# Layer norm by VectorE statistics, gated-attention scores two levels to a PSUM bank, and operand addresses uniform modulo 256

## The chip, the cores and the metric

The kernel runs on one core of a Trainium2 chip. The metric is the time of one execution on the device, in microseconds; runs are compared by their median. TensorE (PE in the profile) has two clock levels, 1.2 and 2.4 GHz; the profile gives the granted clock as a share of the higher one.

## What is computed

Two transformer blocks on 256 tokens of width 1024, in float32. The first block has three small attentions whose outputs are gated and merged, and a convolutional feed-forward network. The second has a gated linear attention (GLA), a layer norm, a dilated sliding-window attention and a second layer norm. The two parts that the change rewrites are these:

```python
def layer_norm(x, g, b):
    mu = jnp.mean(x32, axis=-1, keepdims=True)
    xc = x32 - mu
    var = jnp.mean(xc * xc, axis=-1, keepdims=True)
    return xc * lax.rsqrt(var + LN_EPS) * g + b

def gla_chunked(q, k, v, log_a):
    ...
        diff = bc[:, :, :, None, :] - bc[:, :, None, :, :]
        decay = jnp.where(causal, jnp.exp(jnp.where(causal, diff, 0.0)), 0.0)
        att = jnp.einsum('bhid,bhjd,bhijd->bhij', qc, kc, decay)
    ...

def second_block(x, ...):
    ...
        x = layer_norm(DEEPNORM_ALPHA * x + y, ln_g[layer], ln_b[layer])
```

## The kernel before

**Products.** Every large product is made of three float32r matmuls (`mm3`, L271): each operand is split into a high and a low part, and the three are high times low, low times high and high times high. Weights come from memory through one stream (`Stream`, L103): SP loads 1 MB into `raw`, ACT rounds 1024 columns into `whi` (L158) and VectorE (DVE) subtracts to get `wlo` (L159). Both have six buffers. Where a weight is the stationary operand (keys in `STILL`, L36) `wlo` begins 64 bytes into its buffer, otherwise at its start. In those stages 256 columns of activations move (`wstat`, L517, and `wpair`, L522); in `tokmm` (L798) the activation is stationary and 512 columns of weights move.

**Where operands lie.** A `whi` buffer has 4096 bytes per partition, a `wlo` buffer 4224, which is 16.5 times 256, so that successive `wlo` buffers begin at 0 and 128 modulo 256. The split activations of a stage take two buffers from `big8` (L397) of 8320 bytes, 32.5 times 256: one begins at 0 and the other at 128. With the offsets in the code the high and low parts lie, modulo 256 and counted from `whi`, at 0 and 128 for `hhi` and `hlo` (gate projections), at 128 and 0 for `mhi`/`mlo` and `x2hi`/`x2lo`, at 0 and 192 for `h2hi`/`h2lo` (feed-forward up projection), and at 32 and 224 for `x3hi`/`x3lo` (dilated attention). The feed-forward's own `fhi`/`flo` lie at 0 and 0.

**PSUM.** There are eight banks: four of tag `acc` (`acc_t`), two of tag `mm` (`mm_t`) and two of tag `at` (`at_t`). A tile of a tag waits until the tile that last had its bank has been read.

**GLA scores.** `gla_x` (L1012) makes, for a block b and a half u of the eight levels, one PSUM tile per head, which ACT turns into `E` by an exponential (L1024) and DVE multiplies with keys and queries into `Xk` and `Xq`. `gla_p` (L1034) then makes one PSUM tile for each level, and DVE copies it under a mask into `attT` (L1044, L1050). All these tiles have tag `at`. The two generators are advanced between the groups of value and gate projections (L1087 to L1104), which use `acc`. `gla_out(0)` (L1069) takes two `mm` banks.

**Layer norm.** `layer_norm` (L1157) runs over two row blocks b and two halves h of 512 columns. Its order is written out by hand in `ORD3` and `ORD4`, a letter for each step; a `Queue` issues each step of an engine behind the one before it, at high priority, so DVE works the list in order. `u` makes alpha x + y from PSUM with a row sum, `c` the mean (two small operations) and, on ACT, the sum of squares over 1024 columns, `r` adds epsilon on DVE and takes the power on GpSimd (POOL), `w` subtracts the mean and multiplies with g, `n`, `N` and `o` scale (on ACT, on DVE, and on DVE with the bias). The second norm ends the kernel: `o` is followed by the output's DMA for that half.

Of the kernel before, what the change touches and what calls it, by code (L numbers as in the profile page):

```python
# [30 lines left out]
ORD3 = "u00 u01 c0 w00 w01 r0 n00 n01 u10 u11 c1 w10 w11 r1 N10 N11"  # L31
ORD4 = "u00 u01 c0 w00 w01 r0 u10 o00 u11 c1 o01 w10 r1 w11 o10 o11"
SC_SWA = float(128.0 ** -0.5)


STILL = ("in1", "inc", "zg", "br", "up", "gla", "gk", "kvk", "sq")  # L36

# [65 lines left out]
class Stream:  # L103
# [31 lines left out]
    def _chunk(self, i):  # L135
# [13 lines left out]
        for o in range(0, n, part) if part > 0 else range(0, -part, 1024):  # L149
            m = min(part, n - o) if part > 0 else min(1024, -part - o)  # L150
            hi = self.pool.tile([128, 1024], F32R, tag="whi", name="whi", bufs=self.hlbufs)
            lo = self.pool.tile([128, 1056], F32R, tag="wlo", name="wlo", bufs=self.hlbufs)
# [78 lines left out]
def hybrid_blocks(ctx, tc, A, out, dbg=None):  # L231
# [124 lines left out]
    def junk():  # L356
        return cn.tile([128, D], BF, name="junk", tag="junk")
# [39 lines left out]
    def big8(dt, name, past=0):  # L397
        t = cn.tile([128, KK * S + 32], dt, name=name, tag="big8r", bufs=2)
        return t[:, past:past + KK * S].rearrange("p (k s) -> p k s", k=KK)

    hT = (big8(F32R, "hhi"), big8(F32R, "hlo"))
# [224 lines left out]
    yT = (p1.tile([128, 6, S], F32R, name="yhi", tag="yhi"), p1.tile([128, 6, S], F32R, name="ylo", tag="ylo"))  # L626
# [278 lines left out]
    res, _ = open_pool("res")  # L905
    ctx.callback(_)
# [9 lines left out]
    h2 = (big8(F32R, "h2hi"), big8(F32R, "h2lo", 16))  # L916
# [95 lines left out]
    def gla_x(b, u):  # L1012
# [5 lines left out]
        for h in range(4):  # L1018
            pm = at_t()
# [14 lines left out]
    def gla_p(b, u):  # L1034

        Xk, Xq = XK[b, u]
        for l in range(4):
            pp = at_t()
            if 4 * u + l < 7:
                n = 64 >> (4 * u + l)  # L1040
                late = lambda x: x.rearrange("p (g t s) -> p g t s", t=2, s=n)[:, :, 1, :]
                for h in range(4):
                    mm(pp[:, h * 64:(h + 1) * 64].rearrange("p (g s) -> p g s", s=n), Xk[:, h, l, :], late(Xq[:, h, l, :]), True, True)
                dve.copy_predicated(attT[:, 2 * b].rearrange("p h (g t s) -> p h g t s", t=2, s=n)[:, :, :, 1, :],  # L1044
                                    late(glamask[:, 4 * u + l, :])[:, None].to_broadcast([128, 4, 64 // n, n]),
                                    pp[:, 0:256].rearrange("p (h g s) -> p h g s", h=4, s=n))
                continue
            for h in range(4):
                mm(pp[:, h * 128:(h + 1) * 128], kT[:, h, b * 128:(b + 1) * 128], qT[:, h, b * 128:(b + 1) * 128], True, True)
            dve.copy_predicated(attT[:, 2 * b], glamask[:, 4 * u + l, :][:, None, :].to_broadcast([128, 4, 128]),  # L1050
                                pp.rearrange("p (h q) -> p h q", h=4))
# [105 lines left out]
    def layer_norm(x, y, grow, brow, dst, utile, order, after=None):  # L1157
# [3 lines left out]
        su, r, u, w = {}, {}, {}, {}  # L1161
        with tc.high_priority(BOOST):
            for step in order.split():
                op, b, h = step[0], int(step[1]), int(step[2:] or 0)
                c = half(h)
                if op == "u":
                    if not h:
                        su[b] = cn.tile([128, 6], F32, name="su", tag="su", bufs=2)
                        u[b], w[b] = utile(b), utile(b + 2)
                    qd.scalar_tensor_tensor(u[b][:, c], x[:, b, c], ALPHA, y[b][h], op0=OP.mult, op1=OP.add, accum_out=su[b][:, h:h + 1])  # L1170
                elif op == "c":
                    qd.tensor_scalar(su[b][:, 2:3], su[b][:, 0:1], su[b][:, 1:2], -1.0 / (32.0 * D), op0=OP.add, op1=OP.mult)
                    qd.tensor_scalar(su[b][:, 3:4], su[b][:, 2:3], -32.0, None, op0=OP.mult)
                    qa.activation(junk(), u[b], AF.Square, bias=su[b][:, 2:3], scale=1.0 / 32.0, accum_out=su[b][:, 4:5])
                elif op == "w":
                    qd.scalar_tensor_tensor(w[b][:, c], u[b][:, c], su[b][:, 3:4], grow[:, c], op0=OP.subtract, op1=OP.mult)
                elif op == "r":
                    r[b] = rstd(su[b][:, 4:5], 1, 1e-5, qd)
# [265 lines left out]
```

## Time and profile before

| what | value |
|---|---|
| median of 3 runs | 736.43 us (734.82 to 740.46) |
| the profiled execution | 733.62 us, of which its span 731.6 us |
| PE, DVE, ACT, POOL busy | 96%, 75%, 56%, 3% of the span |
| granted clock, mean | 0.986 |

The span runs from the first to the last instruction. PE's busy time counts overlapping matmuls once; their ends are modelled, so that the pace of matmuls is read from the distance of their starts.

### The profile page before, as it was taken

The page shows a single profiled execution, that of the slowest core. Times are in us where ns is not written, and L with a number is a line of the kernel's source. Part 1 is how long each engine was busy: PE and PEld are TensorE (multiplying, and loading weights), DVE is VectorE, ACT ScalarE, POOL GpSimd, SP SyncE. Part 2 cuts the span into 40 slices and gives each one's busy share as a digit, 9 for nine tenths or more (in the row PEclk, how much of TensorE's full clock was granted, in tenths as well). Part 3 has the DMA queues.
Part 4 walks back from the last instruction along what each step waited for, and adds up shares of the span by engine and source line. Part 5 has one row for each costly group of instructions (what it writes and reads, how often), then busy time and mean ns, then how long its engine had stood idle before and what let it go on. Part 6 is the DMA issues. An engine that isn't in the chain of part 4 may idle for free. (4 is left out here: it accounts for less than half of the span.)

```text
span 731.6 us, 12192 instructions
## 1 busy us (share of the span) xinstructions
PE 700.6 (96%) x4878; PEld 636.4 (87%) x4878; DVE 547.1 (75%) x933; ACT 407.1 (56%) x675; POOL 20.2 (3%) x34
## 2 busy tenths in 40 slices
PE   4999999999979999999999899999989999999995
PEld 4888888998859999998999797888879999999984
DVE  5877969898868776768566756675777689777866
ACT  3447788546548555554545774543555556555542
POOL 0001000000010000000000200001010000000000
PEclk8999999999999999999999999999999999999999
DMA  8996768677734765758554464231437755433201
GB/s 321 418 345 237 275 257 301 229 250 255 256 136 174 276 243 178 262 207 310 201 195 174 181 224 141 109 116 58 189 142 276 261 194 168 168 125 135 89 1 57
DMA packets 24600, 148.74 MB, mean 203 GB/s; under 512 B 2992, under 2 KB 3248, under 8 KB 9568
## 3 DMA queue, kind: packets, MB, share of 16 engines
q1 hardware_dynamic: 21888, 139.05, 52.1%
q0 software_dynamic: 1280, 5.18, 2.1%
q10 hardware_dynamic: 1376, 3.74, 1.5%
q8 instruction: 38, 0.62, 0.3%
q14 instruction: 18, 0.15, 0.1%
HBM read 145.86 MB, written 2.10 MB: 202 GB/s over the span
## 5 line engine op out<-in xcount | busy, mean ns | idle before, releaser
L159 DVE TENSOR_TENSOR wlo<-raw,whi 128x1024 fp32r<-128x1024 f32 (+1 forms) x193 | 231.3, 1210 | 63.1 <-ACT whi L158 63.1
L158 ACT ACTIVATE whi<-raw 128x1024 fp32r<-128x1024 f32 (+1 forms) x193 | 199.4, 1050 | 94.1 <-PE acc L262 42.5
L262 PE MATMUL mm<-h2hi,wlo 128*128 128x256 f32 x352 | 98.3, 280 | 0.0
L262 PE MATMUL mm<-h2hi,whi 128*128 128x256 f32 x352 | 98.1, 280 | 0.0
L262 PE MATMUL mm<-h2lo,whi 128*128 128x256 f32 x352 | 97.0, 282 | 0.0
L262 PE MATMUL mm<-x3hi,wlo 128*128 128x256 f32 x304 | 86.2, 285 | 0.0
L262 PE MATMUL mm<-x3hi,whi 128*128 128x256 f32 x304 | 85.1, 281 | 0.0
L262 PE MATMUL mm<-x3lo,whi 128*128 128x256 f32 x304 | 82.9, 280 | 0.0
L262 PEld LDWEIGHTS mm<-h2hi,wlo 128*128 128x128 f32 x352 | 67.0, 190 | 0.4
L262 PEld LDWEIGHTS mm<-h2hi,whi 128*128 128x128 f32 x352 | 66.9, 190 | 0.0
L262 PEld LDWEIGHTS mm<-h2lo,whi 128*128 128x128 f32 x352 | 65.1, 188 | 0.3
L262 PE MATMUL mm<-hhi,wlo 128*128 128x256 f32 x208 | 59.5, 286 | 0.5 <-DVE wlo L159 0.3
L262 PE MATMUL mm<-hlo,whi 128*128 128x256 f32 x208 | 59.2, 285 | 0.0
L262 PE MATMUL mm<-hhi,whi 128*128 128x256 f32 x208 | 58.7, 282 | 0.0
L262 PEld LDWEIGHTS mm<-x3hi,wlo 128*128 128x128 f32 x304 | 57.7, 190 | 0.0
L262 PEld LDWEIGHTS mm<-x3hi,whi 128*128 128x128 f32 x304 | 57.5, 189 | 0.0
L262 PEld LDWEIGHTS mm<-x3lo,whi 128*128 128x128 f32 x304 | 56.2, 188 | 0.0
L262 PEld LDWEIGHTS mm<-hhi,wlo 128*128 128x128 f32 x208 | 39.0, 188 | 2.5 <-PE mm L262 0.8
L262 PEld LDWEIGHTS mm<-hlo,whi 128*128 128x128 f32 x208 | 39.1, 188 | 0.8 <-issue 0.8
L262 PEld LDWEIGHTS mm<-hhi,whi 128*128 128x128 f32 x208 | 39.1, 188 | 0.6 <-issue 0.5
L445 DVE SCALAR_TENSOR_TENSOR adacc<-raw,cact,adacc 128x1024 f32<-128x1024 f32 x28 | 35.7, 1276 | 0.2
L262 PE MATMUL acc<-whi,flo 128*128 128x512 f32 x88 | 34.8, 395 | 0.0
(355 smaller groups left out, 1604.0 us busy)
## 6 DMA issues: line engine op xcount, KB each, us to landing
raw<-in_w_up_dram SPq DMA_DIRECT2D x22, 1024.0 KB, 4.9
raw<-in_w_ada_dram SPq DMA_DIRECT2D x16, 1024.0 KB, 4.9
raw<-in_swa_q_dram SPq DMA_DIRECT2D x16, 1024.0 KB, 4.9
raw<-in_w_zg_dram SPq DMA_DIRECT2D x12, 1024.0 KB, 4.9
raw<-in_w_dn_dram SPq DMA_DIRECT2D x11, 1024.0 KB, 4.7
raw<-in_w_ada_dram SPq DMA_DIRECT2D x16, 512.0 KB, 9.0
early<-in_w_in_dram SPq DMA_DIRECT2D x8, 1024.0 KB, 7.3
raw<-in_gla_vg_dram SPq DMA_DIRECT2D x8, 1024.0 KB, 5.1
```

Of the source, the lines that this page charges most:

```text
L158: i0 = nc.scalar.activation(hi[:, :m], raw[:, o:o + m], AF.Copy)
L159: i1 = nc.vector.tensor_sub(lo[:, :m], raw[:, o:o + m], hi[:, :m].bitcast(F32))
L262: return pe.matmul(o, l, r, start=start, stop=stop, skip_group_check=share)
L445: dve.scalar_tensor_tensor(a, w, c, a, op0=OP.mult, op1=OP.add)
```

## The change

1. `layer_norm` drops the row sums, the small mean operations and ACT's squares. A new step `v` runs `bn_stats` on DVE over each half of u, and `c` becomes one `bn_aggr` over the two, whose mean and variance `w` and `r` read. `ORD3` and `ORD4` are rewritten: each `u` is followed by its `v`, `r` comes ahead of the `w` steps, one N of the first norm's second block moves to ACT, and in `ORD4` both `o` of the first block come ahead of the second block's `u11`.
2. `gla_x` puts every second head's tile into an `mm` bank. `gla_p` puts two levels into one bank, the first two levels into an `at` and the others into an `mm` bank, issues all matmuls first and the masked copies after.
3. Buffer sizes become multiples of 256 bytes: `wlo` 4352, `big8` 8448, `yhi`/`ylo` 6400. High parts begin at their buffer's start, low parts of `h`, `y`, `h2` and `x3` 192 bytes (`PAST` = 48 elements) into theirs.
4. The pool `res`, which holds `x2`, is closed ahead of `p4`, so that the last stage's tiles lie lower.

```diff
-ORD3 = "u00 u01 c0 w00 w01 r0 n00 n01 u10 u11 c1 w10 w11 r1 N10 N11"
-ORD4 = "u00 u01 c0 w00 w01 r0 u10 o00 u11 c1 o01 w10 r1 w11 o10 o11"
+ORD3 = "u00 v00 u01 v01 c0 r0 w00 w01 n00 n01 u10 v10 u11 v11 c1 r1 w10 n10 w11 N11"
+ORD4 = "u00 v00 u01 v01 c0 r0 w00 w01 u10 v10 o00 o01 u11 v11 c1 r1 w10 w11 o10 o11"
+PAST = 48
-            lo = self.pool.tile([128, 1056], F32R, tag="wlo", name="wlo", bufs=self.hlbufs)
+            lo = self.pool.tile([128, 1088], F32R, tag="wlo", name="wlo", bufs=self.hlbufs)
-        t = cn.tile([128, KK * S + 32], dt, name=name, tag="big8r", bufs=2)
+        t = cn.tile([128, KK * S + 64], dt, name=name, tag="big8r", bufs=2)
-    hT = (big8(F32R, "hhi"), big8(F32R, "hlo"))
+    hT = (big8(F32R, "hhi"), big8(F32R, "hlo", PAST))
-    yT = (p1.tile([128, 6, S], F32R, name="yhi", tag="yhi"), p1.tile([128, 6, S], F32R, name="ylo", tag="ylo"))
+    yT = tuple(p1.tile([128, 6 * S + 64], F32R, name=n, tag=n)[:, q:q + 6 * S].rearrange("p (k s) -> p k s", k=6)
+               for n, q in (("yhi", 0), ("ylo", PAST)))
-    h2 = (big8(F32R, "h2hi"), big8(F32R, "h2lo", 16))
+    h2 = (big8(F32R, "h2hi"), big8(F32R, "h2lo", PAST))
...
-            pm = at_t()
+            pm = mm_t() if h % 2 else at_t()
...
+        levels = [l for l in range(4) if 4 * u + l < 7]
+        banks = [mm_t() if i else at_t() for i in range(2)]
+        for l in levels:
+            n = 64 >> (4 * u + l)
             for h in range(4):
+                o = banks[l // 2][:, l % 2 * 256 + h * 64:l % 2 * 256 + (h + 1) * 64]
+                mm(o.rearrange("p (g s) -> p g s", s=n), Xk[:, h, l, :], late(Xq[:, h, l, :], n), True, True)
...
                 if op == "u":
-                        su[b] = cn.tile([128, 6], F32, name="su", tag="su", bufs=2)
+                        st[b] = cn.tile([128, 16], F32, name="lns", tag="lns", bufs=2)
-                    qd.scalar_tensor_tensor(u[b][:, c], x[:, b, c], ALPHA, y[b][h], op0=OP.mult, op1=OP.add, accum_out=su[b][:, h:h + 1])
+                    qd.scalar_tensor_tensor(u[b][:, c], x[:, b, c], ALPHA, y[b][h], op0=OP.mult, op1=OP.add)
+                elif op == "v":
+                    qd.bn_stats(st[b][:, 6 * h:6 * h + 6], u[b][:, c])
                 elif op == "c":
-                    qd.tensor_scalar(su[b][:, 2:3], su[b][:, 0:1], su[b][:, 1:2], -1.0 / (32.0 * D), op0=OP.add, op1=OP.mult)
-                    qd.tensor_scalar(su[b][:, 3:4], su[b][:, 2:3], -32.0, None, op0=OP.mult)
-                    qa.activation(junk(), u[b], AF.Square, bias=su[b][:, 2:3], scale=1.0 / 32.0, accum_out=su[b][:, 4:5])
+                    qd.bn_aggr(st[b][:, 12:14], st[b][:, 0:12])
                 elif op == "w":
-                    qd.scalar_tensor_tensor(w[b][:, c], u[b][:, c], su[b][:, 3:4], grow[:, c], op0=OP.subtract, op1=OP.mult)
+                    qd.scalar_tensor_tensor(w[b][:, c], u[b][:, c], st[b][:, 12:13], grow[:, c], op0=OP.subtract, op1=OP.mult)
                 elif op == "r":
-                    r[b] = rstd(su[b][:, 4:5], 1, 1e-5, qd)
+                    r[b] = rstd(st[b][:, 13:14], 1, 1e-5, qd)
...
-    x3T = (big8(F32R, "x3hi", 8), big8(F32R, "x3lo", 24))
+    x3T = (big8(F32R, "x3hi"), big8(F32R, "x3lo", PAST))
...
     close_p3()
+    close_res()
     p4, close_p4 = open_pool("p4")
```

## Rows read from the trace of the kernel before

**Rows 1.** The page's head and its part 1: busy time of each engine.

```profile
span 731.6 us, 12192 instructions
PE 700.6 (96%) x4878; PEld 636.4 (87%) x4878; DVE 547.1 (75%) x933; ACT 407.1 (56%) x675; POOL 20.2 (3%) x34
```

**Rows 2.** Stretches: us, busy (x) of PE, PEld, DVE, ACT, POOL; PEclk, DMA.

```profile
224.00:404.00 180.00, 180.00 (x1299) 168.78 (x1298) 127.12 (x170) 96.33 (x137) 1.66 (x3) 1.00 0.62 225
541.00:543.00 2.00, 1.87 (x9) 1.87 (x10) 0.74 (x3) 1.14 (x4) 0.00 (x0) 0.50 0.78 244
```

**Rows 3.** Timeline of PE, up and down projections: start, duration, line, operation.

```profile
282.74 0.28 PE L262 MATMUL mm<-h2lo,whi 128*128 128x256 f32 x1
...
288.17 0.40 PE L262 MATMUL acc<-whi,flo 128*128 128x512 f32 x1
...
292.95 0.39 PE L262 MATMUL acc<-whi,flo 128*128 128x512 f32 x1
```

**Rows 4.** Chain that ended last: start, us, what (dilated attention, value projection, transposes).

```profile
438.49 5.57 PE acc L262 x24
...
601.73 0.87 PE at L1282 x8
602.61 5.67 PE mm L262 x48
```

**Rows 5.** Timeline of PE, the first block's output projection.

```profile
206.53 0.40 PE L262 MATMUL acc<-wlo,mhi 128*128 128x512 f32 x1
...
213.01 0.39 PE L262 MATMUL acc<-whi,mhi 128*128 128x512 f32 x1
```

**Rows 6.** Timeline of PE in the GLA stage; in brackets idle time before, and releaser.

```profile
447.11 0.50 PE L262 MATMUL at<-glamr,Ll 128*128 128x512 f32 x1 [1.22 <-ACT E L1024]
...
497.90 1.11 PE L262 MATMUL at<-Xq,Xk 128*128 128x64 f32 x8 [0.33 <-DVE attT L1044]
...
507.62 1.04 PE L193 MATMUL mm<-ident,sg 128*128 128x128 f32 x8
```

**Rows 7.** Chain that ended last, in the same stage.

```profile
445.16 1.28 ACT L1024
...
495.95 1.05 POOL rs L364
```

**Rows 8.** Timeline of all engines around the first layer norm's second block.

```profile
537.27 0.69 DVE L193 SCALAR_TENSOR_TENSOR lnu<-x,acc 128x512 f32<-128x512 f32 x1 [2.04 <-PE acc L262]
...
538.31 1.15 ACT L193 ACTIVATE junk<-lnu,su 128x1024 bf16<-128x1024 f32 x1 [1.86 <-DVE su L193]
...
540.00 0.55 POOL L364 TENSOR_TENSOR rs<-ms,mhalf 128x1 f32<-128x1 f32 x1 [4.92 <-DVE ms L193]
540.59 0.88 DVE L193 TENSOR_SCALAR x<-lnw,rs 128x512 f32<-128x512 f32 x2 [0.67 <-POOL rs L364]
...
541.13 1.97 PE L890 MATMUL acc<-ident,x 128*128 128x128 f32 x8 [2.66 <-DVE x L193]
```

**Rows 9.** Timeline of DVE over the second layer norm, to the last operation.

```profile
718.71 0.69 DVE L193 SCALAR_TENSOR_TENSOR lnu<-x3p,acc 128x512 f32<-128x512 f32 x1 [0.77 <-PE acc L193]
...
720.14 0.40 DVE L193 TENSOR_SCALAR su<-su 128x1 f32<-128x1 f32 x2
...
723.53 0.69 DVE L193 SCALAR_TENSOR_TENSOR lnu<-x3p,acc 128x512 f32<-128x512 f32 x1
724.14 0.08 DVE L193 DVE_READ_ACCUMULATOR lnu<-x3p,acc 128x1 f32 x1
...
727.15 1.41 DVE L193 SCALAR_TENSOR_TENSOR x3p<-lnw,rs,r_lnb 128x512 f32<-128x512 f32 x2 [0.44 <-POOL rs L364]
```

**Rows 10.** Groups of DVE by shape: count, busy us, mean ns of one, idle before.

```profile
L159 DVE TENSOR_TENSOR wlo<-raw,whi 128x1024 fp32r<-128x1024 f32 x185 | 223.7, 1221 | 62.9 <-ACT whi L158 62.9
...
L1269 DVE TENSOR_SCALAR sP<-sP,sst 128x512 f32<-128x512 f32 x16 | 7.7, 485 | 0.4
...
L393 DVE TENSOR_REDUCE ssq<-sq 128x256 f32<-128x512 f32 x4 | 2.8, 698 | 3.9 <-ACT sq L391 3.9
```

More of the change, by code (lines that the diff above doesn't have):

```diff
@@ L904, in hybrid_blocks @@
     close_p1a()
-    res, _ = open_pool("res")
-    ctx.callback(_)
+    res, close_res = open_pool("res")
     p2, close_p2 = open_pool("p2")
@@ L1036, in gla_p @@
         Xk, Xq = XK[b, u]
[L1037 to L1047, printed above, removed]
-            for h in range(4):
-                mm(pp[:, h * 128:(h + 1) * 128], kT[:, h, b * 128:(b + 1) * 128], qT[:, h, b * 128:(b + 1) * 128], True, True)
-            dve.copy_predicated(attT[:, 2 * b], glamask[:, 4 * u + l, :][:, None, :].to_broadcast([128, 4, 128]),
-                                pp.rearrange("p (h q) -> p h q", h=4))
+        late = lambda x, n: x.rearrange("p (g t s) -> p g t s", t=2, s=n)[:, :, 1, :]
@@ new lines, in gla_p @@
+        levels = [l for l in range(4) if 4 * u + l < 7]
+        banks = [mm_t() if i else at_t() for i in range(2)]
+        for l in levels:
+            n = 64 >> (4 * u + l)
+            for h in range(4):
+                o = banks[l // 2][:, l % 2 * 256 + h * 64:l % 2 * 256 + (h + 1) * 64]
+                mm(o.rearrange("p (g s) -> p g s", s=n), Xk[:, h, l, :], late(Xq[:, h, l, :], n), True, True)
+        if u:
+            pd = at_t()
+            for h in range(4):
+                mm(pd[:, h * 128:(h + 1) * 128], kT[:, h, b * 128:(b + 1) * 128], qT[:, h, b * 128:(b + 1) * 128], True, True)
@@ new lines, in gla_p @@
+        for l in levels:
+            n = 64 >> (4 * u + l)
+            dve.copy_predicated(attT[:, 2 * b].rearrange("p h (g t s) -> p h g t s", t=2, s=n)[:, :, :, 1, :],
+                                late(glamask[:, 4 * u + l, :], n)[:, None].to_broadcast([128, 4, 64 // n, n]),
+                                banks[l // 2][:, l % 2 * 256:l % 2 * 256 + 256].rearrange("p (h g s) -> p h g s", h=4, s=n))
+        if u:
+            dve.copy_predicated(attT[:, 2 * b], glamask[:, 7, :][:, None, :].to_broadcast([128, 4, 128]),
+                                pd.rearrange("p (h q) -> p h q", h=4))
@@ L1160, in layer_norm @@
         qa, qd = Queue(tc, act, ws.last[0]), Queue(tc, dve, ws.last[1])
-        su, r, u, w = {}, {}, {}, {}
+        st, r, u, w = {}, {}, {}, {}
         with tc.high_priority(BOOST):
```

## The prediction

> **What bounds the kernel now.** I read the page first: PE is busy 96% of a span of 731.6 us, DVE 75% [rows 1]. Then the busy time by stretches: over the 180 us of the feed-forward network PE is busy without a gap at the full clock while DVE has 53 us to spare [rows 2]. So in most of the span the pace of matmuls sets the time, and nothing that DVE or ACT saves there is worth anything. Third I read the timeline of PE for that pace, and last the few places where PE stands idle: in the GLA stage [rows 6, 7], around the first layer norm [rows 8] and behind the last matmul, where DVE runs alone to the end [rows 9]. The change touches all four, and each part goes by its own limit.
>
> **Addresses: the pace of matmuls.** The pace differs from stage to stage though the matmuls are alike. In the up projection 47 matmuls of 256 columns run from 282.74 to 288.17, 115.5 ns each [rows 3]. In the dilated attention 48 of the same shape take 5.67 us, 118.1 ns [rows 4]. The same holds with 512 columns: 21 of the down projection from 288.17 to 292.95, 227.6 ns each [rows 3]; 28 of the output projection from 206.53 to 213.01, 231.4 ns [rows 5]; 24 of GLA's value projection in 5.57 us, 232.1 ns [rows 4]. What differs between them, by the code, is where the operands begin modulo 256: the shorter pace belongs to stages whose high part lies in phase with `whi` (`h2` at 0 and 192, `f` at 0 and 0), the longer pace to those at 32 and 224 (`x3`) or at 128 and 0 (`m`, `x2`). The profile has no address in it, so this is an inference from these stages.
>
> The change puts `x3` at 0 and 192, as `h2` was, and `m` and `x2` at 0 and 0, as `f` was. Priced by the rows of the shorter pace: the dilated attention has 19 weight tiles of 48 matmuls (three of keys, sixteen of queries and gates), 912 x 2.6 ns = 2.4 us; GLA's value and gate projections 192 x 4.5 ns = 0.9 us; the output projection 96 x 3.8 ns = 0.4 us. Together -3.6 us. The up projection keeps its phases and I count nothing there; the gate and branch projections, the down projection and the two remaining output projections change by amounts that I can't separate and leave at nothing.
>
> One thing in the code counts the other way. The new statistics tile (16 numbers, 64 bytes, two buffers) lies in the pool of small tiles in front of everything, so all large operands move up by 128 bytes. Their positions relative to each other stay as designed, but none of them begins at a multiple of 256 any more. I take the relative phase as what counts, since each stage's rows can be told apart by it; if the absolute address counts, the stages at 115.5 ns lose (a rival below). The bounds of this term are therefore -10 us (a pace halfway to the 109 ns of the transposes, whose eight took 0.87 us [rows 4]) and +4.4 us.
>
> Here a rule speaks against the change. The trace has different paces for equal shapes [rows 3, 4]. The Trainium skill, in "TensorE: Matmul & The Clock Gate", section Part 2, says that PE reads the moving operand and the next weights through two independent ports, so that loading weights takes no bandwidth from the running matmul. By that rule addresses would not matter, this term would be 0 and the sum below -0.1 us; the rows only show that something other than shape sets the pace.
>
> **GLA scores in four banks.** PE idles twice for want of an `at` bank. At 447.11 the third head's tile waits 1.22 us until ACT, after a table load of 1.28 us, has read the first [rows 6, 7]. With heads alternating over `at` and `mm` the four tiles need no release, and that wait goes. What is late next is DVE's first products from `E`, which still come after the same table load; PE has more of the value projection to run in between, so I take 0.9 of the 1.22 us. At 497.90 PE waits 0.33 us for a masked copy [rows 6]; DVE had that copy queued behind the scaling of `gla_out(0)`, which waits for POOL's power of 1.05 us [rows 7]. With copies behind all matmuls, and `gla_out(0)` after them because it needs `mm` banks that the scores now hold, this goes too: 0.3 us. Together -1.2 us. The cost to watch is that same `mm` dependence: squares, power and scaling of block 0 come later, and behind them DVE's gating and the transposes at 507.62 [rows 6]. PE has a projection's rest and `gla_out(1)` in between, so I price it at nothing; without that cover it costs up to the POOL and scaling time, some 2 us. Bounds: -1.6 to +2.
>
> **First layer norm.** PE waits for the second block. Before: `u11` starts at 537.27, the two mean operations follow, ACT's squares start at 538.31 and take 1.15 us, DVE scales from 540.59 and the transposes start at 541.13 [rows 8]. After: `u11` 0.70, its `bn_stats` 0.73, then the aggregate and epsilon at 0.2 each, the price of one of the two mean operations [rows 9], which is 539.1; POOL's power of 0.55 us [rows 8] runs beside `w10`, and ACT scales the first half from about 539.8 to 540.5. The transposes start near 540.5, -0.6 us. That half moves to ACT's queue, where a row load and the evacuation of the transposes stand behind it; the evacuation waits for the transposes anyway. For `bn_stats` there is no row. The nearest is a reduction that reads 512 elements, 698 ns; below it a scalar operation, 485 ns; above, if it passed twice over the data, an operation on 1024 columns, 1221 ns [rows 10]. I take 0.70, by the reduction, which also reads one tensor and writes little. Ahead of `u11` DVE had 2.04 us idle [rows 8]; the list there grows by three `bn_stats` with their waits (2.3) and loses three accumulator reads and a small step (0.4), so 1.9 of the 2.04 is used and `u11` isn't late. With 1.22 it would be late by 1.4, and the norm would cost +1.3; with 0.49 it gives -0.8. PE's clock was at 0.50 from 541 to 543 because PE had stood still [rows 2]; a shorter pause may spare that, up to 0.5 us, which I leave out.
>
> **Second layer norm: the tail.** Here DVE alone sets the end. From `u00` at 718.71 to the end of the last `o` at 727.15 + 1.41 = 728.56 it works 9.85 us, with 0.44 us of waiting [rows 9]. `u11` started at 723.53, just as its bank came free, so DVE was already as late as PE. The change adds four `bn_stats` (4 x 0.70 = 2.8), drops four reads of accumulators (4 x 0.08), halves the two mean steps (2 x 0.2) and the wait for POOL (0.44), since `r` now comes ahead of two `w`; ACT's squares, which ran beside DVE, are now DVE's. 2.8 - 0.32 - 0.4 - 0.44 = 1.64, and each `bn_stats` must wait out its `u` in full where before independent operations overlapped by some 0.07: +1.7 us. Seen from the list: `u11` stands behind three `bn_stats` and both `o` of block 0 and starts near 725.9, not 723.53, and behind it lie 4.5 us of DVE. The output's DMAs of block 0 leave from SP ahead of `u11`, where nothing else is left to issue, and the last one still follows the last `o`. Bounds by the same rows: +0.8 and +3.8.
>
> **The rest.** Closing `res` early moves `p4` lower; the first tile written there waits for `x2`'s last reader, which is the first layer norm, over before. Nothing. Splits on DVE and ACT have the same count.
>
> **Sum.** -3.6 - 1.2 - 0.6 + 1.7 = -3.7 us on the profiled span: 727.9. That execution took 733.62 us, 2.8 under the median of 736.43; from the median, 732.7.
>
> **Rivals.** (1) Addresses do nothing: -0.1, 736.3. For it: no row has an address; against: the paces sort by phase. 15%. (2) The common shift of 128 hurts, the case on the slower side: the 1680 matmuls of the gate and up projections fall from 115.5 to 118.1 ns, +4.4, `x3` gains nothing, and with the other parts' -0.1 the time is 740.7. It decides as soon as these matmuls lose more than 0.1 us in all, if the others gain nothing. 12%. (3) `bn_stats` passes twice: tail +3.8, first norm +1.3, so +0.3 in all, 736.7. Against it: one-tensor reductions take one pass. 10%. (4) Uniform `wlo` and aligned `whi` make every stage faster than any row shows, halfway to 109 ns: 1680 x 3.2 ns = 5.4 more, and 912 x 3.2 = 2.9 more; 724.4. For it: 109 ns exists; against: `h2` was already in the new phase. 10%. The forecast has the other 53%.
>
> **How the numbers follow.** 1% of the median, about what a measurement can tell from no change, is 7.4 us: 729.1 and 743.8. The forecast lies inside, with a lower tail past 729.1 (8%), (1) and (3) lie inside, (4) outside below, and (2) outside above only if its price is almost doubled (with the unnamed, 7%). So faster 18%, same 75%, slower 7%. The range reaches from the middle between the forecast and (4) past (1) and (3), 727.0 to 738.5; (2) and most of (4) are left out. The forecast's own range, where (1), (3) and it all mean no difference, is 729.5 to 735.5.
>
> **What would show it.** Addresses: 48 matmuls of the dilated attention in about 5.54 us, not 5.67; the up projection still at 115.5 ns. If that one rises to 118, rival (2); if both stand, (1). GLA: no idle of 1.2 us before the third head's tile, and no new idle before the transposes of `sg`. First norm: transposes about 3.3 us after `u11` starts (3.86 before). Tail: `u11` starts over 2 us after its bank is ready, and 11.5 us from `u00` to the last `o`. The prediction is wrong if the matmuls' pace changes in stages that I hold fixed, or if the order of PE's list in GLA comes out otherwise.

## The result: slower by 0.8%, and the rows of the profile after

The changed kernel takes 742.12 us (median; 738.2 to 746.33) where the kernel before takes 736.75: a ratio of 1.0077, interval 1.0063 to 1.0092. The forecast was 732.7 us and its range ended at 738.5, so it was wrong by 9.4 us and on the wrong side. In lines of the code, L262 of before is L264 of after, L193 is L195.

The page's head of the kernel after:

```profile
span 740.9 us, 12181 instructions
PE 710.0 (96%) x4878; PEld 648.6 (88%) x4878; DVE 551.8 (74%) x928; ACT 403.2 (54%) x668; POOL 21.5 (3%) x34
```

PE is busy for 710.0 us where it was 700.6 [rows 1], with the same 4878 matmuls, and idle for 31 us in both: the time went into the matmuls, not into waits. The timeline of PE in the up projection (start, duration, line, operation) shows where:

```profile
287.74 0.29 PE L264 MATMUL mm<-h2lo,whi 128*128 128x256 f32 x1
...
289.06 0.28 PE L264 MATMUL mm<-h2hi,wlo 128*128 128x256 f32 x1
...
291.58 0.28 PE L264 MATMUL mm<-h2hi,wlo 128*128 128x256 f32 x1
...
293.50 0.29 PE L264 MATMUL mm<-h2lo,whi 128*128 128x256 f32 x1
```

From the first to the last of these lie 48 matmuls: 5.76 us, 120.0 ns each, where 115.5 ns was read [rows 3]. This is a stage at which I had counted nothing. The chain that ended last, in the GLA's value projection and the dilated attention of the kernel after:

```profile
465.45 5.46 PE acc L264 x24
...
584.11 16.65 PE mm L264 x144
...
602.52 5.76 PE mm L264 x48
608.28 0.87 PE at L1290 x8
609.15 5.76 PE mm L264 x48
```

The 512-column matmuls went the way that I forecast, 24 in 5.46 us, 227.5 ns each, against 5.57 [rows 4]; the 256-column ones of `x3`, forecast at 5.54 us for 48, went from 5.67 [rows 4] to 5.76. But not all of them: at 584.11 the first three tiles of queries and gates take 16.65 us for 144 matmuls, 115.6 ns each. By the built program they read the same six buffers of weights, at the same addresses, as the tiles behind them. So this kernel has both paces at the same addresses.

By stages (worked out from the starts of records; us). A stage runs from its first matmul to the first of the next; a norm begins at the last product ahead of it:

| stage | before | after | difference |
|---|---|---|---|
| first block to its output projection | 169.55 | 176.00 | +6.45 |
| output projection and residual norm | 31.11 | 30.98 | -0.13 |
| feed-forward | 185.16 | 189.16 | +4.00 |
| second residual norm | 4.02 | 4.01 | 0 |
| GLA | 127.16 | 124.25 | -2.91 |
| first layer norm | 5.91 | 5.16 | -0.75 |
| dilated attention to its last product | 180.35 | 182.16 | +1.81 |
| behind it to the end | 8.50 | 10.28 | +1.78 |

The two profiled executions lie 9.3 us apart, the medians only 5.4, so the table holds some 4 us that belong to these executions. Much of that lies in the first block. Stretches (us, busy time and count of PE, PEld, DVE, ACT, POOL; PEclk, DMA), first of the kernel before, then two of the kernel after:

```profile
30.00:189.00 159.00, 156.26 (x1234) 141.34 (x1233) 138.50 (x279) 102.17 (x206) 3.66 (x6) 1.00 0.75 276
...
90.90:94.30 3.40, 3.19 (x15) 3.19 (x16) 3.40 (x14) 3.16 (x9) 0.00 (x0) 0.50 0.76 317
135.30:138.70 3.40, 3.40 (x18) 3.40 (x17) 3.40 (x10) 0.12 (x1) 0.00 (x0) 0.50 0.93 352
```

The kernel before had the full clock (1.00) through the whole stretch; the kernel after had the lower level (0.50) twice. The first time PE stood idle for 2.87 us around the fall, where the kernel before stood idle for 1.21. The timeline of PE, before and after:

```profile
89.33 0.33 PE L687 MATMUL at<-ident,Pat 128*128 128x128 f32 x1 [1.21 <-ACT Pat L679]
...
91.11 0.48 PE L690 MATMUL at<-ident,Pat 128*128 128x128 f32 x1 [2.87 <-ACT Pat L682]
```

The kernel before moved up by 128 bytes, below, has such a stretch from 134.1 too, at the old pace and with a first block of 172.53 us. So this part isn't shown to come from the change.

### The profile page after: what moved, and what is told of

It is laid out like the page before. It is cut to its first block, busy times and chain, and to the rows that moved or that the text cites. A ratio compares the mean times of both kernels' runs of the same rounds, so it can differ in the third digit from the quotient of the medians.

```text
span 740.9 us, 12181 instructions
## 1 busy us (share of the span) xinstructions
PE 710.0 (96%) x4878; PEld 648.6 (88%) x4878; DVE 551.8 (74%) x928; ACT 403.2 (54%) x668; POOL 21.5 (3%) x34
## 5 line engine op out<-in xcount | busy, mean ns | idle before, releaser
L264 PE MATMUL mm<-h2hi,whi 128*128 128x256 f32 x352 | 99.2, 283 | 0.0
L264 PE MATMUL mm<-h2hi,wlo 128*128 128x256 f32 x352 | 99.1, 283 | 0.0
L264 PE MATMUL mm<-h2lo,whi 128*128 128x256 f32 x352 | 98.2, 286 | 0.0
L264 PE MATMUL mm<-x3hi,wlo 128*128 128x256 f32 x304 | 87.5, 289 | 0.0
L264 PE MATMUL mm<-x3hi,whi 128*128 128x256 f32 x304 | 86.5, 286 | 0.0
L264 PE MATMUL mm<-x3lo,whi 128*128 128x256 f32 x304 | 84.3, 285 | 0.0
L264 PEld LDWEIGHTS mm<-h2hi,whi 128*128 128x128 f32 x352 | 67.1, 191 | 0.0
L264 PEld LDWEIGHTS mm<-h2hi,wlo 128*128 128x128 f32 x352 | 66.8, 190 | 0.4
L264 PEld LDWEIGHTS mm<-h2lo,whi 128*128 128x128 f32 x352 | 65.3, 188 | 0.3
L264 PE MATMUL mm<-hhi,wlo 128*128 128x256 f32 x208 | 61.4, 295 | 0.5 <-DVE st L677 0.5
L264 PE MATMUL mm<-hlo,whi 128*128 128x256 f32 x208 | 60.9, 293 | 0.0
L264 PE MATMUL mm<-hhi,whi 128*128 128x256 f32 x208 | 60.8, 292 | 0.0
L264 PEld LDWEIGHTS mm<-x3hi,whi 128*128 128x128 f32 x304 | 58.9, 194 | 0.0
L264 PEld LDWEIGHTS mm<-x3hi,wlo 128*128 128x128 f32 x304 | 58.5, 192 | 0.1
L264 PEld LDWEIGHTS mm<-x3lo,whi 128*128 128x128 f32 x304 | 56.8, 190 | 0.0
L264 PEld LDWEIGHTS mm<-hhi,wlo 128*128 128x128 f32 x208 | 40.5, 195 | 2.5 <-issue 0.9
L264 PEld LDWEIGHTS mm<-hlo,whi 128*128 128x128 f32 x208 | 41.0, 197 | 0.8 <-issue 0.8
L264 PEld LDWEIGHTS mm<-hhi,whi 128*128 128x128 f32 x208 | 40.8, 196 | 0.6 <-issue 0.5
L264 PE MATMUL acc<-whi,flo 128*128 128x512 f32 x88 | 34.7, 394 | 0.0
```

The source lines that it names most:

```text
L264: return pe.matmul(o, l, r, start=start, stop=stop, skip_group_check=share)
```

## Experiments

Matmuls come in groups of three (high on low weight, low on high, high on high). "Pace" below is the median time of such a group in ns, from start to start of records; `h` stands for the gate and first projections, `x3` for the dilated attention's keys, queries and gates. Addresses are those of the built programs; the profile has none. Ratios are to the kernel before on the same chip. A median hides one thing: in each kernel with 360 under `x3`, the 48 groups of the first three tiles of queries and gates pace 347.

| kernel | h | h2 | y | x3 | m (512 columns) | us | ratio, interval |
|---|---|---|---|---|---|---|---|
| before | 347 | 347 | 353 | 354 | 696 | 736.75 | 1 |
| after | 360 | 360 | 360 | 360 | 680 | 742.12 | 1.0077, 1.0063 to 1.0092 |
| a_base0 | 360 | 360 | 360 | 360 | 680 | 740.75 | 1.0056, 1.0036 to 1.0077 |
| a_step512 | 360 | 360 | 360 | 360 | 680 | 742.65 | 1.0085, 1.0062 to 1.0109 |
| b_shift128 | 347 | 347 | 353 | 354 | 696 | 738.0 | 1.0015, 0.9997 to 1.0033 |
| b_ln | 347 | 347 | 354 | 354 | 695 | 738.74 | 1.0025, 0.9997 to 1.0053 |
| a_c256 | 360 | 360 | 360 | 360 | 680 | 742.38 | 1.0072, 1.0044 to 1.0100 |
| b_c256 | 347 | 347 | 353 | 353 | 696 | 736.26 | 0.9998, 0.9972 to 1.0023 |
| b_gla | 347 | 347 | 353 | 354 | 696 | 733.98 | 0.9965, 0.9934 to 0.9995 |
| a_wlo192 | 347 | 347 | 347 | 347 | 680 | 733.04 | 0.9942, 0.9916 to 0.9967 |
| a_alt | 360 and 347 | 347 | 347 | 347 (358 in one of six buffers) | 686 | 734.63 | 0.9962, 0.9935 to 0.9989 |
| b_addr | 360 | 360 | 360 | 360 | 680 | 742.85 | 1.0082, 1.0056 to 1.0109 |
| a_kick | 360 | 360 | 360 | 360 | 680 | 743.85 | 1.0096, 1.0065 to 1.0128 |
| a_w192_n2 | 347 | 347 | 347 | 347 | 680 | 732.39 | 0.9927, 0.9903 to 0.9952 |

### Where the buffers start, and how far the two activation parts lie apart

**The changed kernel with its base back at 0 modulo 256** (the small statistics tiles put where dead ones lay):

```diff
-    st[b] = cn.tile([128, 16], F32, name="lns", tag="lns", bufs=2)
+    st[b] = cn.tile([128, 16], F32, name="lns", tag=("bgh", "bad1")[b])
```

> The changed kernel with its two statistics tiles put into two small tiles that are free by then, so that nothing moves: all large operands lie 128 bytes lower than in the changed kernel, the high parts and whi at 0 modulo 256 again, all distances between buffers as in the changed kernel. Theory A (where an operand begins modulo 256 counts by itself): the up projection falls from 120.0 to 115.5 ns per matmul, the dilated attention to the same, the gate projections too; about 1000 groups of three matmuls by 13 ns, some 13 us less, 729 us. Theory B (the distance between the low and the high part counts, modulo 512: 192 in the up projection before, 448 after): all stay at 120.0 ns, 742 us.

Measured: 360 stays. The absolute start is not it.

**The changed kernel with activation buffers of 8704 bytes**, so that high and low part lie another distance apart modulo 512 (the scratch row shrinks to make room):

```diff
-    t = cn.tile([128, KK * S + 64], dt, name=name, tag="big8r", bufs=2)
+    t = cn.tile([128, KK * S + 128], dt, name=name, tag="big8r", bufs=2)
...
```

> The changed kernel with the buffers of the split activations enlarged by another 256 bytes (8704, a multiple of 512, and 6656 for y), so that the low part lies 192 modulo 512 from the high part and not 448; the squares' scratch tile is halved for the room. All operands still begin 128 off a multiple of 256. Theory A: stays at 120.0 ns and 742 us. Theory B: 115.5 ns in the gate, up and dilated-attention stages, about 729 us.

Measured: 360 stays; that distance is not it either.

**The kernel before, everything moved up by 128 bytes**, which was my rival (2) by itself:

```diff
-    cols = sm.tile([128, NCOL], F32, name="cols")
+    cols = sm.tile([128, NCOL + 32], F32, name="cols")[:, 0:NCOL]
...
```

> The kernel before with 128 bytes of padding in the pool of small tiles, so that every large operand moves up by 128 bytes and no distance changes; the pool of x2 is closed early for the room. Theory A: the up and gate projections rise from 115.5 towards 120.0 ns, 7 us in all, about 744 us. Theory B: 115.5 ns as before, 737 us, and the early closing of the pool costs nothing.

Measured: no pace changes, and 0.15% lies within what this can tell from nothing. The common shift costs nothing, and `res` closed early, which this kernel shares, neither.

**The kernel before with the new layer norms alone** (the added `v` steps and both new orders; their tiles lie in dead ones, so no address moves):

> The kernel before with the new layer norms alone, their statistics in small tiles that are free, so that no address moves. By the rows of the changed kernel: from the first u to the last o of the second norm 11.5 us instead of 9.85 (+1.7), and about -0.6 in the first norm if the clock behind it stays as it was: +1.1 us, 737.8. The rival, that the norms carry the whole loss: 742.

Measured: +1.8 us by the ratio (-0.2 to +3.9), where +1.1 was expected and 0 is not excluded. The norms don't carry the loss.

### High part against high weights, modulo 512; the GLA alone

**The changed kernel with weights 256 bytes nearer to the activations:**

```diff
-    return cn.tile([128, D], BF, name="junk", tag="junk")
+    return cn.tile([128, D - 128], BF, name="junk", tag="junk")
...
```

> The changed kernel with the norms' statistics tile in tiles that are dead by then and the scratch row for squares cut from 2048 to 1792 bytes: everything that follows it, the split weights first, moves down by 256 bytes against the activation buffers; no other distance changes. Activation and weight high parts then stand 256 bytes apart modulo 512, as in the kernel before, and not 0. Theory C (that distance sets the pace of the 256-column groups): three matmuls take 347 ns in the gate projection and the feed-forward's first half (360 in the kernel after), about 350 in the key and query projection, and y's group stays at 360, because its buffer moves with the weights; some 900 groups of 12 ns, so about -11 us: 730 us, between the kernel before and 728. Theory D (the low parts' stride of 4352 bytes, or the common address of low parts, sets the pace): 360 stays, 741 us.

**The kernel before with them 256 bytes farther** (`D + 128` in the same line, and `res` closed early for the room):

> The kernel before with its scratch row widened from 2048 to 2304 bytes and one small pool closed earlier: split weights and all that follows move up by 256 bytes against the activation buffers; no other distance changes. Activation and weight high parts then stand 0 bytes apart modulo 512. Theory C: three 256-column matmuls go from 347 to 360 ns in the gate projection and the feed-forward's first half, y, key and query groups change by a few ns either way; some 600 groups of 13 ns, +7 us: about 744 us. Theory D: 347 stays, 736.5 us.

Measured: both kept their pace, 360 and 347. Theory C falls from both sides. What all kernels at 360 still share is the uniform start of the low weights.

**The kernel before with the GLA part alone:**

> The kernel before with the GLA part of the change alone: two levels of scores to a bank, the banks taken from two rings in turn; no address moves. What the changed kernel's trace showed beyond the pace of 512-column matmuls is -2.0 us in this stage: 734.5 us. If the GLA's gain was itself one of addresses: 736.5 us. My prediction's term was -1.2 us.

Measured: 733.98 us, 0.9965, which is -2.6 us. The interval only just excludes 0, but the GLA's stage in the trace is 2.1 us shorter (125.06 against 127.16), and no address moved: the gain is no matter of addresses.

**A bare loop over distances** (64 groups a block, 21 blocks, nothing else running but DVE's reading of the banks):

```python
for k in range(8):
    ...
    for x, (m, w) in enumerate(((hi, wlo), (lo, whi), (hi, whi))):
        pe.matmul(q, lhsT=w[:, c], rhs=m[:, s], start=k == 0 and x == 0, stop=k == 7 and x == 2)
```

> Leaves out the whole computation: 21 blocks of 64 groups of three 256-column float32r matmuls from the kernel's own order (high activation on low weight, low on high, high on high), with nothing to wait for, over tiles whose distances modulo 512 bytes are set by block. Block 1: high at 256 from the high weights, low at 448, low weights at 64 (as before the change). Blocks 2 to 9: high at 0, 64 ... 448, low always 192 further, low weights at 64. Blocks 10 to 17: high at 256, low at 0, 64 ... 448. Blocks 18 to 21: high at 256, low at 448, low weights at 0, 128, 192, 256. Theory C: 347 ns for three in block 1 and 6, 360 in block 2 (high at 0), the others in between, and blocks 10 to 17 move by 6 ns at most. Theory D: blocks 1 to 17 all alike, and blocks 18 to 21 differ. If neither, and the pace hangs on other engines' traffic, all 21 are alike.

Measured: neither theory. Blocks paced 347, 353, 357, 358 and 360 with nothing to wait for, so the pace is PE's own and not other engines' traffic. With low weights at 0 or 256 the pace went 360, 353, 358, 342 from one group to the next and round again. But block 2, which has the changed kernel's distances modulo 256, paced 347 and not 360. And blocks 1, 6 and 17 run at the very same addresses and paced 347, 360 and 347. The timeline of PE, two starts out of block 1 and two out of block 6:

```profile
20.15 0.28 PE L257 MATMUL mm<-thi,twlo 128*128 128x256 f32 x1
...
35.06 0.28 PE L257 MATMUL mm<-thi,twlo 128*128 128x256 f32 x1
...
132.95 0.28 PE L257 MATMUL mm<-thi,twlo 128*128 128x256 f32 x1
...
147.35 0.28 PE L257 MATMUL mm<-thi,twlo 128*128 128x256 f32 x1
```

43 groups lie between the first two, 346.7 ns each, and 40 between the last two, 360 each. This alone rules out that the addresses decide by themselves.

### The kernels' own addresses in a bare loop

> Leaves out the whole computation: 38 blocks of 32 groups of three 256-column float32r matmuls with nothing to wait for, at the very addresses of the kernels: blocks 1 to 6 at those of the feed-forward's first half in the kernel before, in four kernels that paced 360 ns (the activation's high and low part, first high and low weight buffer: 19200, 27840, 87040, 111680; the kernel after 19328, 27968, 87424, 112064; 19328, 28224, 86912, 111552; 19200, 27840, 87296, 111936) and in one that paced 347, twice over; then the low activation part alone moved on by 512 to 2048 bytes in steps of 256, the high part down, the low weights up and the high weights up, in steps of 256, and the same addresses with the three matmuls in other orders. Theory E (addresses alone, with more than the lowest 9 bits of them): blocks 2 to 5 pace 360 and 1 and 6 347, both times, and the steps of 256 tell whose bits count. Theory F (addresses do not suffice: what other engines and transfers do in the stage, or how a stage begins, decides): blocks 1 to 6 all pace 347, as the first sweep's did at the same addresses modulo 512.

Measured: the first twelve stretches all paced 360, those at the addresses of the kernel before too, and so did the 22 that moved one operand by multiples of 256 bytes. Other orders of the three gave 353 and 360, the two activation parts exchanged 355. So the same addresses pace 347 in the kernel before and 360 here. Theory E falls, and so does F's number, which was 347 for all. What was left is that the pace depends on what went before.

### Does PE keep the pace it is in?

**The bare loop over one set of buffers**, with the low weights' start x and the low activations' start d changed by stretch, and rests and odd matmuls between:

> Leaves out the whole computation: 35 stretches of groups of three 256-column float32r matmuls with nothing to wait for, always over the same buffers; by stretch only the low weights' start (0, 64, 128 or 192 bytes past a multiple of 256, called x) or the low activations' start (called d) changes, and some stretches begin after a rest of the engine or after one odd matmul of 64 to 448 columns. Order: x = 64, 192, 64, 128, 64, 0, 64, 192, 64 with d = 192; then d = 128, 192, 64, 192, 0, 192, 128, 192 with x = 64; d = 128, 192 with x = 192; five with x = 64 after a rest; six with x = 64 after an odd matmul; x = 64 and 192 in turn; two with x = 192 after a rest. Theory G (at x = 64 and d = 192 the pace has two steady states, 347 and 360 ns for three, and keeps the one it is in; x = 192 or d = 128 has the 347 state alone and leaves the engine in it): 360 in the first stretch, 347 at x = 192 and at x = 64 behind it, 353 at x = 128; 347 at d = 128 and at x = 64 behind it; a rest or an odd matmul may bring either. Theory H (no memory; a layout outside the four buffers decides): x = 64, d = 192 paces 360 wherever it stands.

The pace by stretch, in order (worked out from the starts of records):

```
d=192  x: 64   192  64   128  64   0     64   192  64
      ns: 347  347  347  353  353  342 to 361  347  347  347
x=64   d: 128  192  64   192  0    192  128  192
      ns: 347  347  353  360  353  360  353  360
x=192  d: 128 (from 360 before it: 357 354 354 364, then 347)   192: 347
```

At d = 192 and x = 64, without one address changed, the groups pace 347, 353 or 360, depending on what ran ahead of them. The timeline of PE of this loop, from the first rest on (each row of 96 matmuls is 32 groups at d = 192, x = 64; a row of `odd` is the odd matmul, or one of 256 columns behind a rest. A rest is short: 0.21 us idle ahead of the first one's weight load):

```profile
244.22 0.39 PE L271 MATMUL odd<-z 128*128 128x256 f32 x1
244.44 11.68 PE L256 MATMUL mm<-arena 128*128 128x256 f32 x96
256.08 0.39 PE L271 MATMUL odd<-z 128*128 128x256 f32 x1
256.31 11.67 PE L256 MATMUL mm<-arena 128*128 128x256 f32 x96
267.94 0.39 PE L271 MATMUL odd<-z 128*128 128x256 f32 x1
268.17 11.25 PE L256 MATMUL mm<-arena 128*128 128x256 f32 x96
...
312.73 0.22 PE L271 MATMUL odd<-z 128*128 128x128 f32 x1
312.80 11.30 PE L256 MATMUL mm<-arena 128*128 128x256 f32 x96
323.94 0.25 PE L271 MATMUL odd<-z 128*128 128x192 f32 x1
324.02 11.70 PE L256 MATMUL mm<-arena 128*128 128x256 f32 x96
335.57 0.31 PE L271 MATMUL odd<-z 128*128 128x320 f32 x1
335.71 11.68 PE L256 MATMUL mm<-arena 128*128 128x256 f32 x96
347.23 0.34 PE L271 MATMUL odd<-z 128*128 128x384 f32 x1
347.40 11.27 PE L256 MATMUL mm<-arena 128*128 128x256 f32 x96
```

The same 96 matmuls take 11.68, 11.67 and 11.25 us behind three equal rests, 11.30 behind an odd matmul of 128 columns, 11.70 and 11.68 behind 192 and 320, 11.27 behind 384. 11.7 us is the pace of 360, 11.3 that of 347. At x = 192 both stretches behind a rest came back to 347. Theory G as stated missed three things: the first stretch paced 347 and not 360, x = 64 has a third pace of 353, and d = 128 with x = 64, which I held to have 347 alone, paced 353 when it was entered from 360.

**The changed kernel with low weights at 192 instead of 64:**

```diff
-    lo = lo[:, 16:1040] if key[0] in STILL else lo[:, 0:1024]
+    lo = lo[:, 48:1072] if key[0] in STILL else lo[:, 0:1024]
```

> The changed kernel with the low weights of the 256-column stages 192 bytes into their tile instead of 64; every tile and every other address as in the kernel after. Theory G: three matmuls take 347 ns in the gate projection, the feed-forward's first half, the key and query projection and y, where the kernel after takes 360: about 900 groups by 13 ns, -11 us: 731 us, faster than both kernels. Theory H: 360 stays, 742 us.

Measured: 347 in `h`, `h2`, `y` and `x3`, 733.04 us, 0.9942; this one line takes the loss back and ends 4.3 us below the kernel before. The up projection in its timeline of PE, and a query tile in its chain:

```profile
285.01 0.28 PE L264 MATMUL mm<-h2lo,whi 128*128 128x256 f32 x1
...
290.56 0.28 PE L264 MATMUL mm<-h2lo,whi 128*128 128x256 f32 x1
```

```profile
603.84 5.58 PE mm L264 x48
```

48 matmuls lie between the first two, 115.6 ns each, and `x3` has 5.58 us for 48, near the 5.54 that I had forecast for the change.

**The changed kernel with the low weights' tile back at 1056 floats**, so that they start at 64 and 192 in turn:

```diff
-    lo = self.pool.tile([128, 1088], F32R, tag="wlo", name="wlo", bufs=self.hlbufs)
+    lo = self.pool.tile([128, 1056], F32R, tag="wlo", name="wlo", bufs=self.hlbufs)
```

> The changed kernel with the low weights' tile back at 1056 floats, so that the low weights start at 64 and 192 bytes past a multiple of 256 in turn (256-column stages) and at 0 and 128 (512-column stages); the activations' addresses stay as in the kernel after. Theory G: every buffer at 192 brings the 347 state and the next at 64 keeps it: 347 in the gate projection and the feed-forward's first half; the 512-column stages lose their even pace in every second buffer (about 690 for three instead of 680: some 100 groups, +1 us); 732 us. Theory H: 360 stays: 743 us.

Measured: 734.63 us, 0.9962. In the gate projections eight of the thirteen buffers at 64 paced 360 and four 347 (one has too many waits to tell). Behind a buffer at 360 the next one, at 192, mostly had 358 or 359 ns in its first group and 345 to 349 in those after it: x = 192 takes PE out of the 360 state. In the up projection buffers at 64 and at 192 both paced 347. The first low-weight buffer lies at the same address there as in the kernel after, and so do `h2`'s parts and the high weights; the timeline of PE in this kernel, over seven groups of it:

```profile
286.91 0.28 PE L264 MATMUL mm<-h2hi,wlo 128*128 128x256 f32 x1
...
289.34 0.28 PE L264 MATMUL mm<-h2hi,wlo 128*128 128x256 f32 x1
```

2.43 us for seven groups, 347 ns each; the kernel after has 2.52 (289.06 to 291.58 above), 360 each. Same buffers, same addresses, another history: theory G inside the kernel.

### The addresses alone, an odd matmul, and the second norm taken back

**The kernel before with the change of addresses alone:**

> The kernel before with the change of addresses alone (low weights' tiles of 1088 floats, activation buffers of 8448 bytes, low activation parts 192 bytes in); layer norms and GLA as before. Theory G: as in the changed kernel three 256-column matmuls take 360 ns in the gate projection, the feed-forward's first half, y and the key and query projection, 512-column ones 680: the addresses are the whole loss and what the GLA (-2.1 us by the run of that part alone) and the norms give or take stands beside it, so 742 to 744 us, ratio about 1.009. If instead the loss comes from the parts together, it stays near 736.5.

Measured: 742.85 us, 1.0082, with all paces of the kernel after. The addresses are the whole loss: +6.0 us, the GLA -2.6 and the norms +1.8 give +5.2, and the three together measure +5.7. Each of the three is known to about 2 us either way.

**The changed kernel with one odd matmul ahead of each pair of tiles in the up projection:**

```diff
+    if key[0] == "up":
+        mm(p[:, 256:384], a[0][:, 0, 0:128], a[0][:, 0, 0:128], True, True)
```

> The changed kernel, no address moved, with one extra matmul of 128 columns (hi by hi, into the half of the bank that the next group overwrites) ahead of each pair of output tiles of the feed-forward's first half but the first: 21 extra matmuls of some 60 ns, 1.3 us. Theory G (the pace is kept from what went before): the extra matmul can move it, as one of 128 and one of 384 columns did in the bare loop, and the groups after it pace 347 or 353 in all or some of the 21 pairs: up to 44 times 8 groups by 13 ns less, so between 743.5 (no move) and 739 us. Theory H (the addresses alone): 360 in every group and 743.5 us.

Measured: 743.85 us. The pace within the groups changed (118, 123, 119 ns became 120, 121, 119), but their sum stayed at 360. The odd matmul of 128 columns that brought 347 in the bare loop doesn't here; which state a disturbance leads to I can't forecast. This run by itself doesn't tell theory G from theory H; the two paces at the same addresses, in the bare loops and in the kernel after, do.

**The version with low weights at 192 and the second layer norm as it was:**

```diff
-ORD4 = "u00 v00 u01 v01 c0 r0 w00 w01 u10 v10 o00 o01 u11 v11 c1 r1 w10 w11 o10 o11"
+ORD4 = "u00 u01 c0 w00 w01 r0 u10 o00 u11 c1 o01 w10 r1 w11 o10 o11"
```

> The changed kernel with the low weights of the 256-column stages 192 bytes into their tile (which alone gave a ratio of 0.9942 to the kernel before) and the second layer norm as it was before the change (row sums out of VectorE's additions, squares on ScalarE, the earlier order of steps). The changed kernel's tail after the first addition was 1.69 us longer than that of the kernel before (11.54 against 9.85): taking it back gives 731.3 us where the kernel before is at 736.5 (ratio 0.992 to 0.993). If the tail's length is not the norm's doing but the pace of the matmuls ahead of it, nothing is gained: ratio 0.994 to 0.995.

Measured: 732.39 us, 0.9927 (0.9903 to 0.9952): below both kernels, and by the middle of the interval 1.1 us below the version with both new norms, though the two intervals overlap. Its timeline of DVE over the second norm:

```profile
719.28 0.69 DVE L195 SCALAR_TENSOR_TENSOR lnu<-x3p,acc 128x512 f32<-128x512 f32 x1 [0.76 <-PE acc L195]
...
727.66 1.42 DVE L195 SCALAR_TENSOR_TENSOR x3p<-lnw,rs,r_lnb 128x512 f32<-128x512 f32 x2 [0.44 <-POOL rs L366]
```

9.80 us from the first addition to the last operation, as before [rows 9].

## Why the prediction was wrong

**Addresses: -3.6 forecast, +6.0 measured.** The step that failed is "I take the relative phase as what counts", with "The up projection keeps its phases and I count nothing there". The activations did keep their phase to the weights; the low weights went from 64 and 192 in turn to 64 everywhere, and I named that edit only as a possible gain (rival 4). At 64 the pace has more than one steady state, and without buffers at 192 in between the kernel stayed in the one of 360 nearly throughout. Term by term: the up projection, priced at 0, has 352 groups, 352 x 13 ns = +4.6 us (its stage: +4.0). The dilated attention, priced at -2.4, has 304 groups: 256 of them went from 354 to 360 and 48 to 347, in the mean from 353.8 to 357.4 ns, 304 x 3.6 ns = +1.1; the rest of the stage's +1.81 came from the clock (below). The gate and first projections, which I left at nothing, have 304 groups; those without a wait went from 349.6 to 358.6 ns in the mean, 304 x 9 ns = +2.7. The rest of that stage's +6.45 is mostly no pace: PE waited 1.66 us longer at 91.11 and had two stretches at the lower clock, and the stage's length differs by 3 us between executions of equal pace (169.55 in the kernel before, 172.94 with the norms alone, which change nothing there). The 512-column part was right: 680 ns for three in the output projection and in GLA, as forecast, where 696 stood.

The mechanism had a true part. With the low weights at 192 the address term is -4.3 + 2.6 - 1.8 = -3.5 us, against -3.6 forecast, though by another layout: `x3` and `y` gain 7 and 6 ns a group where I had counted 8 (three times 2.6) for `x3` and nothing for `y`. That the two figures agree so closely is in part luck, since the run's own interval is 3.8 us wide.

**Rival (2)** had the stages and the sign, and its 740.7 us was the nearest number on the page. Its cause was wrong: the common shift alone changes no pace.

**The range.** Its lower end, 727.0, is called the middle between the forecast and (4); that middle, of 732.7 and 724.4, is 728.6. The result lies above the range, so nothing hangs on it.

**GLA: -1.2 forecast, -2.6 alone by the ratio** (interval -4.9 to -0.4), and -2.1 between the traces of that kernel and of before. The mechanism was right. The timeline of PE in the kernel after:

```profile
453.19 0.39 PE L264 MATMUL at<-glamr,Ll 128*128 128x512 f32 x1
...
454.09 0.39 PE L264 MATMUL at<-glamr,Ll 128*128 128x512 f32 x1
...
499.28 0.61 PE L264 MATMUL mm<-Xq,Xk 128*128 128x64 f32 x4
...
514.24 1.04 PE L195 MATMUL mm<-ident,sg 128*128 128x128 f32 x8
```

The third head's tile, at 454.09, has no idle time ahead of it where 1.22 stood [rows 6], the wait of 0.33 for a masked copy is gone, and the transposes of `sg` don't wait, so the cost that I feared (up to 2 us) did not come. I was low because I took 0.9 of the 1.22; the rest of the difference I have not itemised.

**First layer norm: -0.6 forecast, -0.75 measured** from the last output matmul to the first of `x3`. The timeline of all engines:

```profile
543.73 0.69 DVE L195 SCALAR_TENSOR_TENSOR lnu<-x,acc 128x512 f32<-128x512 f32 x1 [0.32 <-PE acc L264]
544.45 0.69 DVE L195 BATCH_NORM_STATS2 lns<-lnu 128x6 f32<-128x512 f32 x1
...
545.17 0.21 DVE L195 BATCH_NORM_AGGREGATE lns<-lns 128x2 f32<-128x12 f32 x1
...
545.65 0.99 POOL L366 TENSOR_TENSOR rs<-ms,mhalf 128x1 f32<-128x1 f32 x1 [3.82 <-DVE ms L195]
...
547.45 1.21 PE L893 MATMUL acc<-ident,x 128*128 128x128 f32 x8 [2.55 <-ACT x L195]
```

`bn_stats` takes 0.69 us where I took 0.70, the aggregate 0.21 where I took 0.2: rival (3) falls. But POOL's power took 0.99 here and 0.55 before [rows 8], so the transposes started 3.72 us behind `u11`, not 3.3. The rest of the gain came from the clock: they ran in 1.21 us where 1.97 stood [rows 8], because the half clock began later. It was not saved but moved. Windows of the kernel after (us, busy time and count of PE, PEld, DVE, ACT, POOL; PEclk, DMA):

```profile
229.00:409.00 180.00, 180.00 (x1279) 169.40 (x1278) 125.03 (x166) 94.62 (x131) 1.10 (x2) 1.00 0.62 225
548.40:551.70 3.30, 3.30 (x17) 3.25 (x16) 2.90 (x8) 3.30 (x8) 0.00 (x0) 0.50 0.96 374
```

For 3.3 us the granted clock is 0.50, the lower level, and PE is busy all of it with the first keys of `x3`: 17 matmuls where some 27 fit at 120 ns. In the kernel before the half clock, 540.48 to 543.89, lay on the transposes and on 1.1 us of `x3`. That is (3.3 - 1.1) / 2 = 1.1 us, and the first 24 matmuls of `x3` show it: from the first start to the last 4.26 us, where 3.35 stood. These 0.9 us and the +1.1 of the pace make the dilated attention's +1.81, to 0.2. The first of the two rows also has 1279 matmuls in 180 us where the kernel before had 1299 [rows 2], at the full clock both times.

**Second layer norm: +1.7 forecast, +1.69 measured.** The timeline of DVE:

```profile
726.28 0.69 DVE L195 SCALAR_TENSOR_TENSOR lnu<-x3p,acc 128x512 f32<-128x512 f32 x1 [0.75 <-PE acc L195]
727.00 0.69 DVE L195 BATCH_NORM_STATS2 lns<-lnu 128x6 f32<-128x512 f32 x1
...
733.33 0.68 DVE L195 SCALAR_TENSOR_TENSOR lnu<-x3p,acc 128x512 f32<-128x512 f32 x1
...
736.41 1.41 DVE L195 SCALAR_TENSOR_TENSOR x3p<-lnw,rs,r_lnb 128x512 f32<-128x512 f32 x2
```

From 726.28 to 737.82 are 11.54 us against 9.85 [rows 9]; the wait for POOL is gone, and `u11` starts 7.05 us behind `u00` where it was 4.82.

**The port rule.** The pace of equal shapes goes with where the operands begin: 353 at x = 128, 347 at x = 192, in a loop that waits for nothing. The conclusion that I weighed, that addresses are of no account, is measured wrong. The Trainium skill, "TensorE: Matmul & The Clock Gate", section Part 2, holds that moving operand and next weights are read through two independent ports. The runs don't say whether ports are shared.

## What to carry to other kernels

A pace read from one stage is one of several that its addresses allow, so read it by stage and by buffer, try a new layout in the whole kernel, and count every edit of an address as a loss too until a row excludes it. A layout in which operands take turns can be better than a uniform one, because one buffer can bring PE back to the shorter pace; the best one here was uniform again, at 192. Moving work to the engine that alone sets the end lengthens the end by that work: four statistics of 0.69 us, less what they replaced, cost the last norm 1.69.

## What the runs showed of the hardware that I had not expected

- A stream of weight loads and float32r matmuls of 256 columns has several steady paces at the same addresses, 347, 353 and 360 ns for three, and within a stretch keeps the one it is in for as long as these runs lasted (32 groups and more). Five equal rests led to 360, 360, 347, 347 and 360. What inside PE holds the state, and what decides which one a start picks, stays open.
- Low weights at 192 bytes past a multiple of 256, with the low activations also at 192, brought 347 in `h`, `h2`, `y` and `x3` of two kernels, and took PE out of 360 within two groups (358 or 359, then 345 to 349); with the low activations at 128 it took five.
- At low weights in line with the high ones (x = 0) the pace runs in a cycle of four groups, 360, 353, 358 and 342.
- Matmuls of 512 columns showed no second state: 680 ns for three where both parts of activations and weights are in phase, 687 where the low weights lay 128 bytes off (buffers in turn in the kernel with 1056 floats).
